# Two-layer hybrid trunk on one core: dense moving operands at the bottom of SBUF, weights at its top

## The chip, the cores and the metric

One core of a Trainium2 chip runs the whole program in one launch. The metric is the device time of one execution in microseconds (us). A measurement of the kernel before is the median of 3 runs; a profiled execution is one run more, with a time of its own.

TensorE multiplies a stationary operand (at most 128x128, loaded by LDWEIGHTS) with a moving operand (128 partitions by 512 columns here) into an accumulator in PSUM. VectorE (DVE), ScalarE (ACT) and GpSimd (POOL) do the elementwise work; SyncE (SP) issues the transfers from HBM. SBUF is the working memory of 128 partitions. In this text a place in SBUF is a distance from the bottom of a partition, in KB of 1024 bytes.

## What is computed

T = 512 tokens, width 1024, two layers. Each adds a mixer's output to the residual and then a gated feed-forward block of inner width 2816:

```python
def swiglu(xn, w_gu, w_down):
    gate, up = jnp.split(xn @ w_gu, 2, axis=-1)
    return (jax.nn.silu(gate) * up) @ w_down
...
for layer in range(DEPTH):
    xn = rms_norm(x, norm_mix[layer])
    h = even_mixer(xn, ...) if layer % 2 == 0 else odd_mixer(xn, ...)
    x = x + h
    x = x + swiglu(rms_norm(x, norm_ffn[layer]), ffn_w_gu[layer], ffn_w_down[layer])
```

The even mixer (layer 0) is a short convolution and a chunked gated delta rule; the odd one (layer 1) is a recurrence with 8 heads and an attention part with low-rank queries and values. All is in 32-bit floats.

## The kernel before

**Dense products.** Everything is kept transposed: features on the partitions, tokens on the columns. A weight block of up to 8 x 128 rows by 128 columns is fetched into `wraw` by `Core.weight`, and split into a high part `whi` (rounded to fp32r) and a low part `wlo` (the rest), 512 columns at a time, four buffers of each. An activation is split in the same way into hi and lo. `Core.mm` makes each 128-deep step of a product of three fp32r matmuls: hi by `whi`, lo by `whi`, hi by `wlo`. The weight is the stationary operand and the activation the moving one, with one exception: in the value product of the attention part the weight block moves, and a 128x128 slice of the activation (`f`) is stationary.

**Activations.** `Core.big` hands out tiles of [128, 8, 512] words (16 KB a partition), four in all; a normalized activation takes a pair of them, hi and lo (`norm_begin`), and the mixers use them for other things too. In a feed-forward block one pair holds the block's input and the other is idle until the last down product.

**Feed-forward block (`Core.ffn`).** The 22 inner units of 128 rows go in two halves of 11. For each unit: gate and up, 8 steps of 3 matmuls each; VectorE and ScalarE make silu(gate) x up, and split it into `hi` and `lo`, each a ring of 13 tiles of [128, 512] in the block's own pool. Then the down product of this half: for each of 8 output blocks, 11 steps of 3 matmuls, added to the residual `xres`. Gate and up are thus 1056 matmuls a layer and down is 528. `mixer_out` ahead of it makes the mixer's output projection and `xres`.

**Order.** `Plan` predicts when each operand is ready and which engine is free, and the recorded operations are issued in that order (line 242, `emit`, which is why most operations of VectorE and ScalarE stand at L242 in the profile; matmuls stand at L363, transposes at L367, transfers at L315). It knows sizes and engines, and no addresses.

**Places.** Pools are stacked from the bottom of SBUF in the order in which they are opened: constants (`con`), weights (`wp`), activations (`act`), and on top of these one pool for each phase (`gdn`, `ffn0`, `odd`, `ffn1`), which is freed at the phase's end. In the built program that gives, in KB, with the places after the change beside them:

| tiles | before | after |
|---|---|---|
| `whi`, `wlo` (stationary) | 30 to 46 | 179 to 195 |
| the four `big` tiles (moving) | 46 to 94 and 114 to 130 | 16 to 80 |
| `x2k` (working tiles of DVE and ACT) | 94 to 112 | 195 to 213 |
| phase pools, from | 133 | 80 |
| `hi` and `lo` of the inner units (moving) | 153 to 205 | the idle `big` pair, and 80 to 100 |
| `xres` | 133 to 149 | 100 to 116 |
| `f` of the attention part | 166 to 224 | 112 to 170 |
| `bones` (a constant matrix, stationary) | 138 | 84 |
| `wraw` | 22 to 30 | 171 to 179 |

The input pair of the feed-forward block lies before at 62 to 78 KB (hi) and 114 to 130 KB (lo) in layer 0, and at 46 to 62 KB (hi) and 78 to 94 KB (lo) in layer 1.

Of the kernel before, what the change touches and what calls it, by code (L numbers as in the profile page):

```python
# [8 lines left out]
F32 = mybir.dt.float32  # L9
F32R = mybir.dt.float32r  # L10
I32 = mybir.dt.int32
AF = mybir.ActivationFunctionType
OP = mybir.AluOpType
# [3 lines left out]
T = 512  # L17
D = 1024
KD = D // 128
D_FF = 2816  # L20
KF = D_FF // 128
# [4 lines left out]
class Plan:  # L26
# [6 lines left out]
    def __init__(self, known):  # L33
        self.now = self.started = 0.0
        self.cols = set(range(4))
        self.busy = {e: ([], []) for e in ("V", "A", "G", "D")}
        self.uses, self.last, self.base, self.slots = {}, {}, {}, {}
        self.known = known
        self.keys, self.seen = {}, {}
        self.dense = []  # L40
        self.place = {}
        self.floor = {}
        self.writes, self.reads = {}, {}
# [209 lines left out]
class Core:  # L253
# [4 lines left out]
    def __init__(self, ctx, tc, I, O, first):  # L258

        self.ctx, self.tc, self.nc, self.I, self.O, self.first = ctx, tc, tc.nc, I, O, first  # L260
        self.pools, self.lined, self.odd_row = {}, [], None
        self.plan = Plan(first.plan.seen if first else None)
        self.con = self.pool(ctx, "con")
        self.wp = self.pool(ctx, "wp")
        self.act = self.pool(ctx, "act")
        self.dr = self.pool(ctx, "dr", space=bass.MemoryType.DRAM)
        self.ps = self.pool(ctx, "ps", space=PSUM)
        self.pp, self.banks = None, {}
        self.V, self.A, self.G = (Engine(self, e, n) for e, n in ((self.nc.vector, "V"), (self.nc.scalar, "A"), (self.nc.gpsimd, "G")))
        self.E = Engine(self, None, "E")  # L270
        self.held, self.flying, self.live, self.ops = {}, 0, [], []
        self.cur, self.steps = Stream(None, None, ()), {}
        self.n = 0
        self.fed = KF

    def pool(self, ctx, name, **kw):
        p = ctx.enter_context(self.tc.tile_pool(name=name, bufs=1, **kw))
        self.pools[id(p)] = name
        if not kw and name not in ("gdn", "odd"):
            self.lined.append(p)  # L280
        self.plan.floor[name] = self.plan.end()
        return p
# [5 lines left out]
    def tile(self, pool, shape, dt, tag, bufs=1, name=None, typed=False):  # L288

        cur = self.cur  # L290
        cur.tiles += 1
        slot = (self.pools[id(pool)], tag)
        n = int(np.prod(shape[1:]))
        full = [shape[0], -(-n // self.ROW) * self.ROW] if pool in self.lined and tag not in ("x2k", "half") and n % self.ROW else shape

        def make(i):

            t = pool.tile(full, dt, name=name or self.nm(tag), **({"tag": f"{tag}{i}", "bufs": 1} if typed else {"tag": tag, "bufs": bufs}))[:]
            if full is not shape:
                t = t[:, :n]  # L300
                if len(shape) == 3:
                    t = t.rearrange("p (a b) -> p a b", b=shape[2])
                elif len(shape) == 4:
                    t = t.rearrange("p (a b c) -> p a b c", b=shape[2], c=shape[3])
            return t

        t = self.plan.alloc(slot, bufs, (cur.key, cur.tiles), make, lambda old: self.live and (not typed or old.dtype == dt))
        if self.live and not self.first:
            need = self.steps.setdefault((cur.key, cur.step), {})
            need[slot] = (min(need.get(slot, (0, 0))[0] + 1, bufs), bufs)  # L310
        return t if t.dtype == dt else t.bitcast(dt)
# [11 lines left out]
        else:  # L323
            instr()

    def line(self, pool):

        return self.tile(pool, [128, 8], F32, "half")

    def const(self, name):  # L330
        return self.tile(self.con, list(self.I[name].shape), F32, "c_" + name)

    def big(self, dt=F32):
        return self.tile(self.act, [128, KD, T], dt, "big", 4, typed=True)

    def x2k(self, dt=F32, full=False):
        t = self.tile(self.act, [128, T + 4], dt, "x2k", self.NX)
        if not self.odd_row:
            self.odd_row = self.line(self.act)
        return t if full else t[:, :T]  # L340


# [260 lines left out]
        return rs, self.col  # L603


    def ffn(self, fp, l, xs, xres, done):
        I, V, A = self.I, self.V, self.A
        half = KF // 2
        for f0 in (0, half):
            hs = []  # L610
            for f in range(f0, f0 + half):
                pg = self.do(self.project(I["w_gu"][l, 2 * f], xs, tag="mf"))
                pu = self.do(self.project(I["w_gu"][l, 2 * f + 1], xs, tag="mf"))
                if f == 0:
                    rs, _ = self.do(self.norm_end("mm"))
                g, u, h = self.x2k(), self.x2k(), self.x2k()
                V.tensor_tensor(g, pg, rs[:], op=OP.mult)
                A.activation(g, g, AF.Silu)
                V.tensor_tensor(u, pu, rs[:], op=OP.mult)
                V.tensor_tensor(h, g, u, op=OP.mult)  # L620
                hi = self.tile(fp, [128, T], F32R, "hi", 13)
                lo = self.tile(fp, [128, T], F32R, "lo", 13)
                A.activation(hi[:], h, AF.Copy)
                V.tensor_tensor(lo[:], h, hi[:], op=OP.subtract)
                hs.append((hi[:], lo[:]))
            for c in range(KD):
                ps = self.bank("mf")
                for a, b in ((0, 8), (8, half)):
                    w = self.weight(I["w_down"][l, c][:, (f0 + a) * 128:(f0 + b) * 128], b - a, 128)
                    self.do(self.mm(ps, w, hs[a:b], first=a == 0, last=b == half))  # L630
                V.tensor_tensor(xres[:, c], ps, xres[:, c], op=OP.add)
                if f0:
                    done(c, xres[:, c])
# [1229 lines left out]
def build(tc, I, O):  # L1863
    program(tc, I, O, program(tc, I, O, None))


def program(tc, I, O, first):
    with ExitStack() as ctx:
        c = Core(ctx, tc, I, O, first)
        resid, part = (c.dr.tile([KD, 128, T], F32, name=n) for n in ("resid", "part"))  # L1870

        def mixer_out(fp, l, w, ys, old):

            xres = c.tile(fp, [128, KD, T], F32, "xres")
            xs = c.norm_begin(gf[:, KD * l:KD * l + KD])
            for k in range(KD):
                ps = c.do(c.project(w[k], ys, kt=len(ys), tag="mf", late=k < 2))
                x = c.tile(fp, [128, T], F32, "xold", 2)
                c.dma(x, old[k])
                c.V.tensor_tensor(xres[:, k], ps, x, op=OP.add)  # L1880
                c.norm_add(k, xres[:, k])
            return xres, xs

        gm, c.ident, c.ones, c.mhalf, c.stack, gf = (c.const(n) for n in ("norm_mix", "ident", "ones", "mhalf", "stack", "norm_ffn"))
        c.dma(gm, I["norm_mix"])
        c.G.memset(c.ones, 1.0)
        c.A.activation(c.mhalf, c.ones[:, 0:1], AF.Copy, scale=-0.5)
        ys = c.even(gm[:, 0:KD], {"ident": c.ident, "stack": c.stack, "norm_ffn": gf})
        with ExitStack() as fx:
            fp = c.pool(fx, "ffn0")  # L1890
            c.phase(fx, "ffn0", mf=6)
            xres, xs = mixer_out(fp, 0, I["w_eo"], ys, I["xT"])
            c.rope_tables()
            nxt = []

            def done(k, x):
                if k == 0:
                    nxt.append(c.norm_begin(gm[:, KD:2 * KD]))
                c.norm_add(k, x)
                c.dma(resid[k], x)  # L1900

            c.ffn(fp, 0, xs, xres, done)
        xs = nxt[0]
        ys = c.odd(xs, resid, part)
        with ExitStack() as fx:
            fp = c.pool(fx, "ffn1")
            c.phase(fx, "ffn1", mf=6)
            xres, xs = mixer_out(fp, 1, [I["w_oo"][k][:, 0:512] for k in range(KD)], ys, part)
            c.ffn(fp, 1, xs, xres, lambda k, x: c.dma(O["outT"][k], x))
    return c  # L1910


# [12 lines left out]
```

## Time and profile before

| | us |
|---|---|
| median of 3 runs | 1413.68 |
| lowest and highest | 1409.71, 1416.58 |
| the profiled execution, its own time | 1414.12 |
| its span, from the first to the last instruction | 1412.3 |

How to read it: TensorE is busy for 1351.1 us of the span (96%), VectorE for 869.2, ScalarE for 539.4, GpSimd for 248.3. A matmul's recorded duration overlaps the next one's, and its end is modelled; the interval from one start to the next is read from the timeline. In the names of matmuls, `mfps<-big,whi` is: accumulator, moving operand, stationary operand. `mfps` are the accumulators of the feed-forward phases, `mmps` and `mxps` those of the mixers.

### The profile page before, as it was taken

Reading aid. Unit: us, or ns where it says so; the run is one execution under the profiler, and the core shown is the slowest. Engines: PE = TensorE matmul, PEld = TensorE weight load, DVE = VectorE, ACT = ScalarE, POOL = GpSimd, SP = SyncE. Lnnn points to the kernel's source line nnn. Section 1 sums busy time; section 2 is a strip of 40 time slices with the busy share of each in tenths; the row PEclk is TensorE's granted clock in tenths of the full one; section 3 lists DMA queues with packets and bytes.
Section 4 is the critical chain, followed back from the end, with each engine's and each line's share of the span. In section 5 each row is a group of like instructions: output and inputs, shape, how many; then the busy total and the mean of one; then the engine's idle time right before and its main releaser. Section 6 shows DMA issues by size and latency. Waiting matters only on the chain.

```text
span 1412.3 us, 19643 instructions
## 1 busy us (share of the span) xinstructions
PE 1351.1 (96%) x7526; PEld 1076.5 (76%) x7526; DVE 869.2 (62%) x1653; ACT 539.4 (38%) x1003; POOL 248.3 (18%) x221
## 2 busy tenths in 40 slices
PE   8987899999999999999988979998999999999998
PEld 5766788788888888888756757775688888888887
DVE  6999887656444344444699986786755443344432
ACT  5332454243333233334334244635654332233321
POOL 2456132120000000001234541441020000000000
PEclk9999999999999999999989999999999999999999
DMA  5122011242332332324411220155242232322232
GB/s 162 53 68 75 31 61 57 93 156 90 93 102 82 98 104 90 104 86 133 131 46 60 86 69 24 55 169 166 97 165 90 90 96 87 105 100 94 91 119 84
DMA packets 52799, 132.91 MB, mean 94 GB/s; under 512 B 7520, under 2 KB 15712, under 8 KB 52704
## 3 DMA queue, kind: packets, MB, share of 16 engines
q1 hardware_dynamic: 52704, 131.65, 29.1%
q8 instruction: 59, 0.97, 0.3%
q14 instruction: 36, 0.29, 0.1%
HBM read 121.14 MB, written 10.49 MB: 93 GB/s over the span
## 4 chain that ended last, share of the span: by engine, by line
PE 76%; DVE 16%; ACT 3%; issue 2%; POOL 1%; DMA 1%; SPq 0%; POOLq 0%; DVEq 0%; ACTq 0%
PE mfps L363 56%; PE mmps L363 12%; PE mxps L363 7%; DVE x2k L242 6%; DVE big L242 3%; DVE mem L242 2%; PE mxps L367 2%; ACT x2k L242 1%; DVE ar L242 1%; DVE bk L242 1%; DVE wlo L242 1%; DVE f L242 1%; POOL mem L242 1%; ACT mem L242 1%; DMA big<-in_xT 0%
## 5 line engine op out<-in xcount | busy, mean ns | idle before, releaser
L363 PE MATMUL mfps<-big,whi 128*128 128x512 f32 x1600 | 495.0, 390 | 0.6 <-DVE big L242 0.6
L242 ACT ACTIVATE whi<-wraw 128x512 fp32r<-128x512 f32 (+1 forms) x384 | 238.5, 622 | 517.7 <-PE mfps L363 416.3
L242 DVE TENSOR_TENSOR wlo<-wraw,whi 128x512 fp32r<-128x512 f32 (+1 forms) x344 | 234.1, 681 | 214.4 <-ACT whi L242 212.3
L363 PEld LDWEIGHTS mfps<-big,whi 128*128 128x128 f32 x1600 | 300.3, 188 | 64.9 <-DVE big L242 0.9
L363 PE MATMUL mfps<-big,wlo 128*128 128x512 f32 x800 | 311.4, 390 | 1.5 <-DVE wlo L242 1.5
L363 PE MATMUL mmps<-big,whi 128*128 128x512 f32 x768 | 256.3, 415 | 4.6 <-DVE x2k L242 4.6
L363 PEld LDWEIGHTS mfps<-big,wlo 128*128 128x128 f32 x800 | 150.2, 188 | 34.1 <-DVE wlo L242 1.9
L363 PEld LDWEIGHTS mmps<-big,whi 128*128 128x128 f32 x768 | 139.3, 194 | 38.4 <-issue 9.9
L363 PE MATMUL mmps<-big,wlo 128*128 128x512 f32 x384 | 152.9, 398 | 0.0
L363 PE MATMUL mfps<-lo,whi 128*128 128x512 f32 x352 | 139.0, 395 | 0.0
L363 PE MATMUL mfps<-hi,wlo 128*128 128x512 f32 x352 | 139.0, 395 | 0.0
L363 PE MATMUL mfps<-hi,whi 128*128 128x512 f32 x352 | 138.9, 395 | 0.0
L242 DVE TENSOR_TENSOR x2k<-mfps,rs 128x512 f32<-128x512 f32 x88 | 60.6, 691 | 126.6 <-PE mfps L363 124.2
L242 POOL TENSOR_TENSOR wlo<-wraw,whi 128x512 fp32r<-128x512 f32 x70 | 94.3, 1353 | 129.6 <-ACT whi L242 83.4
L242 POOL TENSOR_TENSOR sqacc<-x2k,sqacc 128x512 f32<-128x512 f32 x21 | 27.6, 1316 | 430.1 <-issue 308.8
L363 PEld LDWEIGHTS mmps<-big,wlo 128*128 128x128 f32 x384 | 73.9, 192 | 17.0
L363 PEld LDWEIGHTS mfps<-lo,whi 128*128 128x128 f32 x352 | 66.0, 187 | 16.1
L363 PEld LDWEIGHTS mfps<-hi,whi 128*128 128x128 f32 x352 | 66.0, 188 | 16.1
L363 PEld LDWEIGHTS mfps<-hi,wlo 128*128 128x128 f32 x352 | 66.0, 188 | 16.1
L242 ACT ACTIVATE x2k<-x2k 128x512 f32<-128x512 f32 x79 | 49.9, 631 | 66.5 <-DVE x2k L242 57.3
L367 PE MATMUL mxps<-c_ident,x2k 128*128 128x128 f32 (+1 forms) x196 | 34.6, 288 | 19.5 <-DVE x2k L242 17.7
L242 DVE TENSOR_TENSOR xres<-mfps,xres 128x512 f32<-128x512 f32 x32 | 22.1, 690 | 47.4 <-PE mfps L363 47.4
(311 smaller groups left out, 1555.7 us busy)
## 6 DMA issues: line engine op xcount, KB each, us to landing
wraw<-in_w_gu SPq DMA_DIRECT2D x88, 512.0 KB, 3.5
wraw<-in_w_down SPq DMA_DIRECT2D x32, 512.0 KB, 3.4
wraw<-in_w_ev SPq DMA_DIRECT2D x30, 512.0 KB, 3.5
wraw<-in_w_od SPq DMA_DIRECT2D x20, 512.0 KB, 3.5
wraw<-in_w_down SPq DMA_DIRECT2D x32, 192.0 KB, 2.3
wraw<-in_w_eo SPq DMA_DIRECT2D x8, 512.0 KB, 3.6
wraw<-in_w_oo SPq DMA_DIRECT2D x16, 256.0 KB, 3.0
big<-in_xT SPq DMA_DIRECT2D x8, 256.0 KB, 6.1
```

The lines of the kernel that those rows point to most:

```text
L242: c.emit(t, lambda: getattr(eng, op)(*a, **kw))
L363: self.emit(t, lambda: self.nc.tensor.matmul(out, lhsT, rhs, **kw))
L367: self.emit(t, lambda: self.nc.tensor.transpose(out, x, ident))
```

## The change

Four edits, all of which move tiles:

1. A pool `mov` is opened first, at the bottom of SBUF, and holds the four `big` tiles. Constants, activations and weights go to the other end (`side="right"`), the weights lowest there.
2. The inner units' rings `hi` and `lo` are no tiles of their own any more. Of their 13 places, the first 8 are the slices of the idle `big` pair and 5 are slices of a new tile `hid` in the block's pool, one for hi and one for lo.
3. `hid` is made in `mixer_out`, before `xres`, so that it lies at the bottom of the block's pool.
4. A filler row next to the `x2k` tiles goes away.

```diff
-        self.con = self.pool(ctx, "con")
-        self.wp = self.pool(ctx, "wp")
-        self.act = self.pool(ctx, "act")
+        self.mov = self.pool(ctx, "mov")
+        self.con = self.pool(ctx, "con", side="right")
+        self.act = self.pool(ctx, "act", side="right")
+        self.wp = self.pool(ctx, "wp", side="right")
...
     def big(self, dt=F32):
-        return self.tile(self.act, [128, KD, T], dt, "big", 4, typed=True)
+        return self.tile(self.mov, [128, KD, T], dt, "big", 4, typed=True)
...
-    def ffn(self, fp, l, xs, xres, done):
+    def ffn(self, fp, l, xs, xres, more, done):
         I, V, A = self.I, self.V, self.A
-        half = KF // 2
+        half, ring = KF // 2, KD + 5
+        hid = [[t[:, k] for k in range(KD)] for t in (self.big(F32R), self.big(F32R))]
+        for part, t in zip(hid, more):
+            part += [t[:, k] for k in range(ring - KD)]
...
-                hi = self.tile(fp, [128, T], F32R, "hi", 13)
-                lo = self.tile(fp, [128, T], F32R, "lo", 13)
-                A.activation(hi[:], h, AF.Copy)
-                V.tensor_tensor(lo[:], h, hi[:], op=OP.subtract)
-                hs.append((hi[:], lo[:]))
+                hi, lo = (part[f % ring] for part in hid)
+                A.activation(hi, h, AF.Copy)
+                V.tensor_tensor(lo, h, hi, op=OP.subtract)
+                hs.append((hi, lo))
...
         def mixer_out(fp, l, w, ys, old):
 
+            more = [c.tile(fp, [128, 5, T], F32R, "hid", 2) for _ in range(2)]
             xres = c.tile(fp, [128, KD, T], F32, "xres")
```

The order of the instructions stays. On TensorE, at the first down product of layer 0, from the last matmul of the last up product on, there stood before (numbers tell buffers apart):

```order
L363 MATMUL mfps_5955<-big_4722,wlo_5964 128x512
L363 MATMUL mfps_6001<-hi_5187,whi_6004 128x512
L363 MATMUL mfps_6001<-lo_5188,whi_6004 128x512
L363 MATMUL mfps_6001<-hi_5187,wlo_6006 128x512
L363 MATMUL mfps_6001<-hi_5268,whi_6004 128x512
```

and there stands now:

```order
L358 MATMUL mfps_5864<-big_4649,wlo_5873 128x512
L358 MATMUL mfps_5908<-big_5023,whi_5911 128x512
L358 MATMUL mfps_5908<-big_5024,whi_5911 128x512
L358 MATMUL mfps_5908<-big_5023,wlo_5913 128x512
L358 MATMUL mfps_5908<-big_5023,whi_5911 128x512
```

Each inner unit is read at the same turn; only the tile that holds it has another name, here one `big` tile for all the hi parts and one for the lo parts. (The lines are shifted by 5, since lines went away above.)

## Rows read from the trace of the kernel before

**Rows 1.** The page's first lines, and its part 4.

```profile
span 1412.3 us, 19643 instructions
PE 1351.1 (96%) x7526; PEld 1076.5 (76%) x7526; DVE 869.2 (62%) x1653; ACT 539.4 (38%) x1003; POOL 248.3 (18%) x221
...
PE 76%; DVE 16%; ACT 3%; issue 2%; POOL 1%; DMA 1%; SPq 0%; POOLq 0%; DVEq 0%; ACTq 0%
PE mfps L363 56%; PE mmps L363 12%; PE mxps L363 7%; DVE x2k L242 6%; DVE big L242 3%; DVE mem L242 2%; PE mxps L367 2%; ACT x2k L242 1%; DVE ar L242 1%; DVE bk L242 1%; DVE wlo L242 1%; DVE f L242 1%; POOL mem L242 1%; ACT mem L242 1%; DMA
```

**Rows 2.** Chain of waits in order of time: start us, us, what, matmuls.

```profile
278.55 50.33 PE mfps L363 x220
337.35 347.31 PE mfps L363 x1507
1021.80 33.34 PE mfps L363 x144
1062.82 345.86 PE mfps L363 x1510
```

**Rows 3.** The page's part 5: groups by line and shape.

```profile
L363 PE MATMUL mfps<-big,whi 128*128 128x512 f32 x1600 | 495.0, 390 | 0.6 <-DVE big L242 0.6
...
L363 PEld LDWEIGHTS mfps<-big,whi 128*128 128x128 f32 x1600 | 300.3, 188 | 64.9 <-DVE big L242 0.9
...
L363 PE MATMUL mfps<-lo,whi 128*128 128x512 f32 x352 | 139.0, 395 | 0.0
```

**Rows 4.** Timeline of TensorE, gate and up, layer 1: start us, us, what, count.

```profile
1099.64 0.61 PE L363 MATMUL mfps<-big,whi 128*128 128x512 f32 x2
...
1139.77 0.61 PE L363 MATMUL mfps<-big,whi 128*128 128x512 f32 x2
```

**Rows 5.** The same view, gate and up, layer 0.

```profile
379.78 0.39 PE L363 MATMUL mfps<-big,wlo 128*128 128x512 f32 x1
...
419.83 0.39 PE L363 MATMUL mfps<-big,whi 128*128 128x512 f32 x1
```

**Rows 6.** The same view, a down product, layer 0.

```profile
449.76 0.39 PE L363 MATMUL mfps<-lo,whi 128*128 128x512 f32 x1
...
489.89 0.39 PE L363 MATMUL mfps<-hi,wlo 128*128 128x512 f32 x1
```

**Rows 7.** The same view, the value product of the attention part.

```profile
944.48 0.39 PE L363 MATMUL mmps<-wlo,f 128*128 128x512 f32 x1
944.72 0.63 PE L363 MATMUL mmps<-whi,f 128*128 128x512 f32 x2
...
947.98 0.39 PE L363 MATMUL mmps<-wlo,f 128*128 128x512 f32 x1
```

**Rows 8.** The same view, two pairs of both far.

```profile
792.74 0.64 PE L363 MATMUL mxps<-f,bones 128*128 128x512 f32 x2
793.23 0.63 PE L363 MATMUL mxps<-big,whi 128*128 128x512 f32 x2
...
800.68 0.63 PE L363 MATMUL mxps<-f,bones 128*128 128x512 f32 x2
801.15 0.63 PE L363 MATMUL mxps<-big,whi 128*128 128x512 f32 x2
```

**Rows 9.** The tile hi: what ACT and DVE do, min/median/max ns.

```profile
L242 ACT ACTIVATE hi<-x2k x44: 616/632/635, 340.8 to 1349.0; 128x512 fp32r<-128x512 f32 x44
L242 DVE TENSOR_TENSOR lo<-x2k,hi x44: 684/692/693, 341.5 to 1349.7; 128x512 fp32r<-128x512 f32 x44
```

**Rows 10.** Timeline of TensorE, short runs in the two mixers.

```profile
178.74 0.62 PE L363 MATMUL mmps<-big,whi 128*128 128x512 f32 x2
...
180.58 0.39 PE L363 MATMUL mmps<-big,wlo 128*128 128x512 f32 x1
...
938.05 0.39 PE L363 MATMUL mmps<-f,wlo 128*128 128x512 f32 x1
...
940.13 0.40 PE L363 MATMUL mmps<-f,wlo 128*128 128x512 f32 x1
```

More of the change, by code (lines that the diff above doesn't have):

```diff
@@ L260, in __init__ @@
         self.ctx, self.tc, self.nc, self.I, self.O, self.first = ctx, tc, tc.nc, I, O, first
-        self.pools, self.lined, self.odd_row = {}, [], None
+        self.pools, self.lined = {}, []
         self.plan = Plan(first.plan.seen if first else None)
-        self.con = self.pool(ctx, "con")
-        self.wp = self.pool(ctx, "wp")
-        self.act = self.pool(ctx, "act")
+        self.mov = self.pool(ctx, "mov")
+        self.con = self.pool(ctx, "con", side="right")
+        self.act = self.pool(ctx, "act", side="right")
+        self.wp = self.pool(ctx, "wp", side="right")
         self.dr = self.pool(ctx, "dr", space=bass.MemoryType.DRAM)
@@ L278, in pool @@
         self.pools[id(p)] = name
-        if not kw and name not in ("gdn", "odd"):
+        if "space" not in kw and name not in ("gdn", "odd"):
             self.lined.append(p)
@@ L293, in tile @@
         n = int(np.prod(shape[1:]))
-        full = [shape[0], -(-n // self.ROW) * self.ROW] if pool in self.lined and tag not in ("x2k", "half") and n % self.ROW else shape
+        full = [shape[0], -(-n // self.ROW) * self.ROW] if pool in self.lined and tag not in ("x2k",) and n % self.ROW else shape
         def make(i):
@@ L324, in emit @@
             instr()
-    def line(self, pool):
-        return self.tile(pool, [128, 8], F32, "half")
     def const(self, name):
@@ L333, in big @@
     def big(self, dt=F32):
-        return self.tile(self.act, [128, KD, T], dt, "big", 4, typed=True)
+        return self.tile(self.mov, [128, KD, T], dt, "big", 4, typed=True)
     def x2k(self, dt=F32, full=False):
         t = self.tile(self.act, [128, T + 4], dt, "x2k", self.NX)
-        if not self.odd_row:
-            self.odd_row = self.line(self.act)
         return t if full else t[:, :T]
@@ L1881, in mixer_out @@
                 c.norm_add(k, xres[:, k])
-            return xres, xs
+            return xres, xs, more
         gm, c.ident, c.ones, c.mhalf, c.stack, gf = (c.const(n) for n in ("norm_mix", "ident", "ones", "mhalf", "stack", "norm_ffn"))
@@ L1891, in program @@
             c.phase(fx, "ffn0", mf=6)
-            xres, xs = mixer_out(fp, 0, I["w_eo"], ys, I["xT"])
+            xres, xs, more = mixer_out(fp, 0, I["w_eo"], ys, I["xT"])
             c.rope_tables()
@@ L1900, in done @@
                 c.dma(resid[k], x)
-            c.ffn(fp, 0, xs, xres, done)
+            c.ffn(fp, 0, xs, xres, more, done)
         xs = nxt[0]
@@ L1907, in program @@
             c.phase(fx, "ffn1", mf=6)
-            xres, xs = mixer_out(fp, 1, [I["w_oo"][k][:, 0:512] for k in range(KD)], ys, part)
-            c.ffn(fp, 1, xs, xres, lambda k, x: c.dma(O["outT"][k], x))
+            xres, xs, more = mixer_out(fp, 1, [I["w_oo"][k][:, 0:512] for k in range(KD)], ys, part)
+            c.ffn(fp, 1, xs, xres, more, lambda k, x: c.dma(O["outT"][k], x))
     return c
```

## The prediction

> **What bounds the kernel now.** Read the page's first and fourth parts first [rows 1]. TensorE is busy for 96% of a span of 1412.3 us, and 76% of the chain of work that ended last is TensorE's. Of that chain, 56% is `mfps`, the accumulators of the two feed-forward blocks and of the two output projections, and 12% is `mmps`, the dense products of the two mixers. Next read the chain in order of time [rows 2]. Two pieces of it are nothing but matmuls: 1507 of them in 347.31 us (layer 0) and 1510 in 345.86 us (layer 1). No other engine and no transfer ends a wait inside either, so in half of the span the time is the number of matmuls times the interval from the start of one to the start of the next. The change keeps the number. Only the interval can move, and that is the quantity to read.
>
> The groups by line give a mean duration of 390 ns to a product with `big` moving and of 395 ns to one with `lo` moving [rows 3]. These durations overlap and their ends are modelled, so they are a hint, not the interval. The timeline of TensorE gives it: take the start of a first and a last row of an unbroken stretch and divide by the matmuls between. Four stretches, all 128x128 by 128x512 in fp32r:
>
> - gate and up of layer 1, moving operands at 46 to 62 KB (hi) and 78 to 94 KB (lo), stationary at 30 to 46 KB: 177 matmuls from 1099.64 to 1139.77, **226.7 ns** each [rows 4].
> - gate and up of layer 0, moving at 62 to 78 KB (hi) and 114 to 130 KB (lo), stationary the same: 175 from 379.78 to 419.83, **228.9 ns** [rows 5].
> - the down product, moving at 153 to 205 KB, stationary the same: 172 from 449.76 to 489.89, **233.3 ns** [rows 6].
> - the value product of the attention part, where the roles are turned round: weights of 30 to 46 KB move, and a slice of `f` at 210 to 220 KB is stationary: 15 from 944.48 to 947.98, **233.3 ns** [rows 7].
>
> I read these so. A dense product whose two operands both lie low takes 226.7 ns; one far operand, of whichever kind, adds 6.6 ns; 228.9 is what comes out when one matmul in three (the lo part) has a far operand, 226.7 + 6.6/3 = 228.9. The border for the moving operand lies between 94 KB, the top of the highest tile that is cheap, and 114 KB. The fourth stretch decides the forecast, because it is the only place where a far stationary operand meets a low moving one for long, and it costs as much as the far moving operand of the third. There is one weaker sign that the two add: the pairs `f,bones` have both operands far (165 KB and more, 138 KB), and two of them take 0.47 and 0.49 us, 235 and 245 ns each [rows 8].
>
> **The change part by part.** The program's instructions are the same, in the same order on every engine; the inner units' tiles have other names, and three instructions of TensorE that only wait, ahead of the first down product, are gone. The down product stands between matmuls without idle time [rows 2], so I cost these at nothing. So the change is a change of places, and there are three kinds.
>
> *The moving operands go down.* `big` lies at 16 to 80 KB, the inner units at 16 to 100 KB (eight of 13 in the idle `big` pair, five in the new tile). All but the last 6 KB are below the 94 KB that are known to be cheap, and those hold the lo parts of three of the 22 inner units, which move in one down matmul of three: 1056/3 x 3/22, 48 matmuls, 0.3 us at most.
>
> *The weights go up.* `whi` and `wlo` move from 30 to 46 KB to 179 to 195 KB. Every dense product loads one of them, so by the fourth stretch each of them pays 6.6 ns. The two moves meet in the down product: the moving operand's 6.6 ns is given back and the stationary one's is taken, 233.3 before and after, gain nothing. In gate and up there is little or nothing to give back, and 6.6 ns to pay.
>
> *The rest.* `x2k` goes up by 101 KB, the phase pools down by 53 KB, for VectorE and ScalarE. Such an operation takes 684 to 693 ns for `lo` and 616 to 635 for `hi` [rows 9]; these spreads of 9 and 19 ns are the room that I give to a place. In the two long pieces such work is hidden behind the matmuls [rows 2], and in the mixers, where the two moves have opposite signs, I take 0, with 1 us either way.
>
> The sum, with 233.3 ns as the interval of each dense product afterwards and 0.39 us for the last matmul of a piece:
>
> - layer 0's long piece: 1506 x 233.3 ns + 0.39 = 351.7 us against 347.31, **+4.4**.
> - layer 1's: 1509 x 233.3 + 0.39 = 352.4 against 345.86, **+6.6**.
> - the output projections' pieces [rows 2]: 219 x 233.3 + 0.39 = 51.5 against 50.33, **+1.2**; 143 x 233.3 + 0.39 = 33.8 against 33.34, **+0.4** (here lo and hi already lie far in part).
> - the mixers: 12% of the chain, 169 us, is `mmps`, at 0.23 us each some 740 matmuls. They stand in short runs after a wait, and there the interval has not settled: with both operands low, 8 matmuls from 178.74 to 180.58 take 230.0 ns each; with a far moving operand, 9 from 938.05 to 940.13 take 231.1 [rows 10]. So the price is between 1.1 ns (0.8 us) and the settled 6.6 ns (4.9 us). The rows nearest to such runs give the lower end, and longer ones come nearer to the upper, so I stay below the middle: **+2.0**.
>
> Together +14.6 us. The profiled execution took 1414.12 us, the median of the runs is 1413.68; on the median that gives **1428.3 us**, 1.0% slower. Three bounds go into the range: the mixers, 0.8 to 4.9 us; the interval after the change, read over 3.50 us with starts to 0.01 us, good to 0.7 ns, which is 2 us over 3015 matmuls; and the products of the attention part with `f`, in which both operands are then far, 120 matmuls, 0.8 us. With the 1 us of the other engines the forecast's own range is 1424 to 1434.
>
> [...]
>
> **The rivals.** [...]
>
> *The place counts for nothing*, and the intervals come from something that the change leaves alone: which accumulator is written, which tile is filled meanwhile, or the order of the three products. Then the time stays at **1413.7 us**. [...] Against it: rows 4 and 5 are the same code on the same shapes with the same engines at work, and differ in the place of the two moving tiles alone.
>
> That the tiles don't go where the change says is excluded by the built program's addresses; that the inner units make a new wait is excluded by its order, since their 13 places are reused in the same turn as before.
>
> **How the numbers follow.** I give the forecast 0.78, the first rival 0.14, the second 0.08. What a measurement of this kernel can tell from no change is about 0.5%, 7 us: the forecast's whole own range (10 us and more above) counts as slower, the first rival (9.7 below) as faster, the second as the same. The range reaches from the forecast down over the second rival to 1412 and up to 1434; it leaves out the first rival and some of the tails, about 0.18.
>
> **What would show it.** Right: the two long pieces of the chain measure some 351.7 and 352.4 us; the mean of `mfps<-big,whi` rises from 390 to about 395 ns while products of the inner units stay at 394 to 396; the timeline of layer 1's gate and up gives 233.3. Wrong: gate and up at 226.7 or less and inner units at 389 or 390 mean that only moving operands count; layer 0 at 228.9 still, with the down product at 233.3, means that places don't count. A new wait in either long piece would mean that the turn of the inner tiles does bind. If gate and up settle between 227 and 233, the price of a far stationary operand was mis-sized.

## The result, and the profile after

The changed kernel takes 1427.87 us (median of 6 runs, 1427.57 to 1429.68), the kernel before 1415.32 us (6 runs, 1409.71 to 1416.74): ratio 1.0096, 95% interval 1.0078 to 1.0114, so 1.0% slower. The forecast was 1428.3 us. The number came out, and so did most terms of its sum. The reason given for it did not: in the experiments below it is not the place of an operand that costs (with the weights as far away, but 64 B lower, the kernel takes 1406.16 us).

The page of the kernel after, its first lines and part 4, against [rows 1]:

```profile
span 1425.8 us, 19643 instructions
PE 1368.5 (96%) x7526; PEld 1078.1 (76%) x7526; DVE 871.8 (61%) x1653; ACT 539.9 (38%) x1003; POOL 249.4 (17%) x221
...
PE 78%; DVE 15%; ACT 3%; issue 2%; DMA 1%; POOL 1%; SPq 0%; POOLq 0%; DVEq 0%; ACTq 0%
```

As many instructions, 13.5 us more span, 17.4 us more recorded busy time on TensorE, the other engines within 3 us of where they were. The granted clock is 0.985 in this execution and 0.986 in that of the kernel before, so the clock is not what changed. The chain of waits of the kernel after, the pieces that answer to [rows 2] (start us, us, what, matmuls):

```profile
279.10 51.60 PE mfps L358 x220
...
339.25 351.63 PE mfps L358 x1507
...
1028.35 33.60 PE mfps L358 x144
...
1069.80 352.34 PE mfps L358 x1510
```

The pieces hold the same numbers of matmuls, so no new wait cuts them. They grew by 1.27, 4.32, 0.26 and 6.48 us, together 12.3 of the 13.5 us. The groups by line and shape, against [rows 3]:

```profile
L358 PE MATMUL mfps<-big,whi 128*128 128x512 f32 x2112 | 664.3, 396 | 0.6 <-DVE big L242 0.6
L358 PEld LDWEIGHTS mfps<-big,whi 128*128 128x128 f32 x2112 | 396.9, 188 | 96.3 <-DVE big L242 0.9
...
L358 PE MATMUL mfps<-hid,whi 128*128 128x512 f32 x192 | 60.7, 396 | 0.0
```

The mean of the products with `big` moving rose from 390 to 396 ns, the load's stayed at 188. The timeline of TensorE after the change (start us, us, what, count) gives the interval: gate and up of layer 1, then of layer 0, then down, then the value product, against [rows 4 to 7]:

```profile
1099.73 0.39 PE L358 MATMUL mfps<-big,wlo 128*128 128x512 f32 x1
...
1139.63 0.40 PE L358 MATMUL mfps<-big,wlo 128*128 128x512 f32 x1
```

```profile
379.68 0.40 PE L358 MATMUL mfps<-big,wlo 128*128 128x512 f32 x1
...
419.58 0.39 PE L358 MATMUL mfps<-big,wlo 128*128 128x512 f32 x1
```

```profile
449.91 0.63 PE L358 MATMUL mfps<-hid,whi 128*128 128x512 f32 x2
...
489.81 0.63 PE L358 MATMUL mfps<-hid,whi 128*128 128x512 f32 x2
```

```profile
950.90 0.39 PE L358 MATMUL mmps<-wlo,f 128*128 128x512 f32 x1
...
954.40 0.39 PE L358 MATMUL mmps<-wlo,f 128*128 128x512 f32 x1
```

171 products in the first three pairs (39.90 us each) and 15 in the last (3.50): 233.3 ns everywhere. The last was the first thing that did not fit. Both its operands now lie far (179 KB and more, and above 112 KB), one more than before, and it still takes 233.3 ns.

Intervals given below are worked out in this way, as the mean over settled triples of the trace; a triple is the three products of one step, hi by `whi`, lo by `whi`, hi by `wlo`.

### The profile page after: what moved, and what is told of

Its sections match the earlier page's. It is cut to its first block, busy times and chain, and to the rows that moved or that the text cites. A ratio compares the mean times of both kernels' runs of the same rounds, so it can differ in the third digit from the quotient of the medians.

```text
span 1425.8 us, 19643 instructions
## 1 busy us (share of the span) xinstructions
PE 1368.5 (96%) x7526; PEld 1078.1 (76%) x7526; DVE 871.8 (61%) x1653; ACT 539.9 (38%) x1003; POOL 249.4 (17%) x221
## 4 chain that ended last, share of the span: by engine, by line
PE 78%; DVE 15%; ACT 3%; issue 2%; DMA 1%; POOL 1%; SPq 0%; POOLq 0%; DVEq 0%; ACTq 0%
PE mfps L358 56%; PE mmps L358 14%; PE mxps L358 7%; DVE x2k L242 6%; DVE big L242 3%; DVE mem L242 2%; PE mxps L362 2%; ACT x2k L242 1%; DVE ar L242 1%; DVE f L242 1%; DVE bk L242 1%; ACT mem L242 1%; DMA qd<-x2k 0%; DMA big<-in_xT 0%; DVE wlo L242 0%
## 5 line engine op out<-in xcount | busy, mean ns | idle before, releaser
L358 PE MATMUL mfps<-big,whi 128*128 128x512 f32 x2112 | 664.3, 396 | 0.6 <-DVE big L242 0.6
L358 PEld LDWEIGHTS mfps<-big,whi 128*128 128x128 f32 x2112 | 396.9, 188 | 96.3 <-DVE big L242 0.9
L358 PE MATMUL mfps<-big,wlo 128*128 128x512 f32 x1056 | 417.5, 396 | 1.4 <-DVE wlo L242 1.4
L358 PEld LDWEIGHTS mfps<-big,wlo 128*128 128x128 f32 x1056 | 198.5, 188 | 49.5 <-DVE wlo L242 1.8
L242 ACT ACTIVATE x2k<-x2k 128x512 f32<-128x512 f32 x79 | 49.9, 632 | 64.8 <-DVE x2k L242 55.5
L358 PE MATMUL mfps<-hid,whi 128*128 128x512 f32 x192 | 60.7, 396 | 0.0
L242 DVE SCALAR_TENSOR_TENSOR x2k<-x2k,conv_qkv,x2k 128x512 f32<-128x512 f32 x54 | 49.9, 924 | 1.6
L362 PEld LDWEIGHTS mxps<-c_ident,x2k 128*128 128x128 f32 (+1 forms) x196 | 23.1, 142 | 33.5 <-DVE x2k L242 23.0
L358 PEld LDWEIGHTS mfps<-hid,whi 128*128 128x128 f32 x192 | 36.1, 188 | 8.7
L242 DVE TENSOR_TENSOR big<-x2k,big 128x512 fp32r<-128x512 f32 x36 | 26.9, 746 | 20.5 <-ACT big L242 20.3
L242 DVE TENSOR_TENSOR x2k<-x2k,x2k 128x512 f32<-128x512 f32 x52 | 37.7, 726 | 1.2 <-ACT x2k L242 1.1
```

Source lines behind the costliest of these rows:

```text
L242: c.emit(t, lambda: getattr(eng, op)(*a, **kw))
L358: self.emit(t, lambda: self.nc.tensor.matmul(out, lhsT, rhs, **kw))
L362: self.emit(t, lambda: self.nc.tensor.transpose(out, x, ident))
```

## The experiments

**Are both operands low enough?** The changed kernel with the weights in a pool of their own at 80 to 96 KB, and `hid` behind it at 96 to 116 KB.

```diff
         self.mov = self.pool(ctx, "mov")
+        self.wst = self.pool(ctx, "wst")
-            hi = self.tile(self.wp, [128, 512], F32R, "whi", 4)
+            hi = self.tile(self.wst, [128, 512], F32R, "whi", 4)
-            lo = self.tile(self.wp, [128, 512], F32R, "wlo", 4)
+            lo = self.tile(self.wst, [128, 512], F32R, "wlo", 4)
```

> The changed kernel with one edit: whi and wlo come from a pool of their own at 80 to 96 KB, just above the big tiles; wraw stays high. Theory (a far operand, the stationary one as well, costs 6.6 ns): gate and up settle at 226.7 ns in both layers, the two long pieces of the chain fall to 341.8 and 342.5 us, and the time is about 1404 us, 24 below the changed kernel and 10 below the kernel before. The down product settles between 226.7 and 233.3: hid now lies at 96 to 116 KB, and its five units of thirteen tell on which side of that the border lies. Rival (weights' place does not count, the 233.3 of the changed kernel comes from the moving operands' new place at the bottom): gate and up stay at 233.3 and the time at 1428 us.

Measured: 1405.49 us (6 runs), ratio to before 0.9932, interval 0.9914 to 0.9950: faster than either kernel. The chain of waits of this kernel, its two long pieces:

```profile
338.62 341.62 PE mfps L359 x1507
...
1057.09 342.32 PE mfps L359 x1510
```

(341.62 - 0.39) / 1506 is 226.6 ns: gate, up and down all run at the short interval, the slices of `hid` at 114 to 116 KB too. This looked like proof of the place. It is also what two other things give, as it turned out.

**Do the weights' places alone make the loss?** The kernel before with its weights' pool on the right, at 208 KB and up; the moving tiles slide down by 24 KB.

```diff
-        self.wp = self.pool(ctx, "wp")
+        self.wp = self.pool(ctx, "wp", side="right")
-        if not kw and name not in ("gdn", "odd"):
+        if "space" not in kw and name not in ("gdn", "odd"):
```

> The kernel before with one edit: the weights' pool alone goes to the top (whi and wlo at 208 to 224 KB); everything else moves down by 24 KB, hi and lo of the inner units lie at 129 to 181 KB. Theory with prices that add: gate and up 233.3 ns, down product 240.0 (both operands far), 1435 us. Theory with one price for a product, whichever of its operands is far: gate and up 233.3, down 233.3, about 1428 us. Rival (the distance between the two operands counts, not the place): gate and up 233.3, but the down product, whose operands are now 27 to 95 KB apart, 227 to 229, about 1420 us.

Measured: 1427.85 us (4 runs), ratio 1.0087, interval 1.0070 to 1.0104: the whole loss. Its two long pieces:

```profile
339.02 351.63 PE mfps L363 x1507
...
1069.10 352.35 PE mfps L363 x1510
```

These are the changed kernel's to 0.01 us, though here the down product has both operands far and there only one. So, in terms of places, a second far operand costs nothing: the prices do not add.

**One weight half low, the other high.** Two runs from the changed kernel, the pool `wst` of the first experiment for `whi` alone, or for `wlo` alone.

```diff
-            hi = self.tile(self.wp, [128, 512], F32R, "whi", 4)
+            hi = self.tile(self.wst, [128, 512], F32R, "whi", 4)
```

> The changed kernel with whi at 80 to 88 KB and wlo left high: one matmul in three has a far stationary operand. If each matmul pays for its own far operand: 226.7 + 6.6/3 = 228.9 ns in gate and up, time about 1413 us. If one far operand in a stretch holds up all three: 233.3 and 1428 us.

> The changed kernel with wlo at 80 to 88 KB and whi left high: two matmuls in three have a far stationary operand. If each matmul pays for its own: 226.7 + 2 x 6.6/3 = 231.1 ns in gate and up, time about 1421 us. If one far operand in a stretch holds up all three: 233.3 and 1428 us.

Measured: 1418.99 us with `whi` low and 1423.18 with `wlo` low (one run each; before's median in the same session 1415.31). The piece of layer 0 in the first, and in the second:

```profile
339.81 348.31 PE mfps L359 x1507
```

```profile
339.00 348.31 PE mfps L359 x1507
```

Both settle at 231.1 ns, whether one load in three is far or two (the 4.2 us between the two runs lie outside the long pieces). A price per far product gives that for two of three, not for one. In these two runs a triple has an interval of its own, which is not the mean of its three products.

**Where is the border?** Two runs. In one the weights lie across the 116 KB that the runs so far suggested, behind the activation tiles, with `whi` from 106016 B and `wlo` from 114208 B. In the other only `hid` is shifted, by 10 KB against the kernel with all low, its low parts to 118912 B and up.

```diff
-        self.act = self.pool(ctx, "act", side="right")
+        self.act = self.pool(ctx, "act")
+        self.wst = self.pool(ctx, "wst")
```

(and `whi` and `wlo` in it, as above)

> The changed kernel, but the weight tiles whi and wlo lie in a pool of their own right after the activation tiles, so that the four whi tiles begin at 106016, 108064, 110112 and 112160 B and the four wlo tiles at 114208, 116256, 118304 and 120352 B; hid comes behind them and lies far, and big and its inner units low as in the changed kernel. Theory (the weight load has the same border as the moving operand, about 116 KB): matmuls whose loaded tile begins at 116256 B or more have a far load, so triples of three of every four steps that share a wlo tile slot, have one far load of three; gate and up come out between the 226.7 ns of all near and the 231.1 ns of one far load in three, about 229 to 230 ns averaged, and the run near 1412 to 1417 us. Rival (the load's border lies elsewhere): below 106 KB, everything 233.3 ns and about 1427 us; between 106 and 114 KB, between 231.1 and 233.3 ns; above 122 KB, gate and up 226.7 ns and about 1406 to 1408 us, since only the down products of hid stay slower.

```diff
+            c.tile(fp, [128, 5, T], F32, "pad")
             more = [c.tile(fp, [128, 5, T], F32R, "hid", 2) for _ in range(2)]
```

> The kernel with all operands low, but with 10 KB unused ahead of hid, whose high parts then lie at 106.1 to 116.1 KB and its low parts from 118912 B up, beyond the border read from the runs so far; the weights stay low. Theory (a moving operand beyond about 116 KB is far): the down triples of the 5 hid units of 22, with one far moving operand of three, go from 226.7 to about 228.9 ns, all else stays at 226.7; that is 192 x 5 / 22 or some 60 triples of 2.2 ns x 3 each a layer, under 1 us in all, so 1405 to 1407 us, and the cadence tells, not the time. Rival (the border lies beyond 126 KB or counts by something else than the address): hid stays at 226.7 ns.

Measured: 1426.03 us and 1405.86 us (one run each, before 1416.45). The first has gate and up at 233.3 ns throughout; the second has `hid` at 226.7 ns up to 126 KB. The groups of the products with `hid` moving, of the first and of the second:

```profile
L359 PE MATMUL mfps<-hid,whi 128*128 128x512 f32 x192 | 60.5, 395 | 0.0
```

```profile
L359 PE MATMUL mfps<-hid,whi 128*128 128x512 f32 x192 | 59.4, 389 | 0.0
```

Both answers went against the theory. Weights from 104 KB up are slow (233.3 ns), moving tiles at 116 to 126 KB are fast (226.7), while in the kernel before moving tiles at 114 KB were slow (228.9) [rows 5]. No border at an address gives that, and the theory of the place was given up. What is left of an address when the place is taken away is its low bits. All fast tiles in all kernels started at a multiple of 128 B (`big` 16512 or 47104 B, weights 82048 or 30720 B), every slow combination had one that did not (117184, 182976, 106016 B).

**Does a start off a multiple of 128 B cost?** Three runs. The column rows `rscol` keep their 32 B, by which, in the kernel before, everything behind them comes 64 B lower and, in the changed one, the weights 64 B higher; in both all tiles then start at multiples of 128 B. The third is the kernel with all low, with the weights (and `hid`) pushed 64 B off, and `rscol` as in the other two.

```diff
-        full = [shape[0], -(-n // self.ROW) * self.ROW] if pool in self.lined and tag not in ("x2k", "half") and n % self.ROW else shape
+        full = [shape[0], -(-n // self.ROW) * self.ROW] if pool in self.lined and tag not in ("x2k", "half", "rscol") and n % self.ROW else shape
```

> The kernel before, but the column rows rscol keep their 32 B each instead of 64 B, so that everything behind them lies 64 B lower: the fourth big tile begins at 117120 B instead of 117184, the inner units from 157056 B on instead of 157120, and all of them now begin at multiples of 128 B, as the near ones always did. Nothing else moves. Theory of the start address (an fp32r operand that begins off a multiple of 128 B costs 6.7 ns a product, wherever it lies): every settled stretch at 226.7 ns, the layer 1 feed-forward piece of the chain 345.9 - 960 x 3 x (228.9 - 226.7) ns = about 341 us with what the down products give back, and 1402 to 1407 us in all. Theory of the place (beyond about 116 KB costs): 64 B change nothing, gate and up 226.7 and 228.9 ns, down 233.3 ns, 1412 to 1417 us.

> The changed kernel with the same edit: rscol lies at the far end of SBUF among the activation rows, and the weights' pool below it rises by 64 B, whi to 183040 B and wlo to 191232 B, both multiples of 128 B, as far away as in the changed kernel. Theory of the start address: 226.7 ns in every settled stretch, layer 0 and layer 1 pieces near 340 us as with all operands low, 1403 to 1408 us. Theory of the place: 233.3 ns throughout and 1426 to 1430 us.

```diff
+        self.gap = self.pool(ctx, "gap")
         self.wst = self.pool(ctx, "wst")
...
+        c.tile(c.gap, [128, 16], F32, "gap")
```

> The kernel with all operands low, but with 64 B unused between the big tiles and the weights, so that whi and wlo begin at 82112 B and 90304 B, 64 B past multiples of 128, as low as before; hid is moved by 64 B with them. Theory of the start address: 233.3 ns in gate and up and in the output projections, 233.3 ns or less in down, 1424 to 1430 us. Theory of the place: 226.7 ns and 1403 to 1409 us.

Measured: 1419.19 us (10 runs, ratio 1.0025, interval 1.0016 to 1.0035), 1427.65 us (5 runs, 1.0080, 1.0055 to 1.0105) and 1426.62 us (one run). The third came out as the start address would have it: 64 B turn a fast kernel, all low, 1405.49 us, into a slow one. The first two did not. With the weights far and at a multiple of 128 B the interval is 232.4 ns, not 226.7 and no longer 233.3; in the kernel before, layer 0's gate and up, at 228.9 ns, went to 231.1 in the first half and to 233.3 in the second. The piece of layer 0 in the first, where it was 347.31 us [rows 2], and in the second:

```profile
339.76 350.10 PE mfps L363 x1507
```

```profile
339.47 350.20 PE mfps L358 x1507
```

The timeline of the first, in the two halves of layer 0's gate and up:

```profile
379.81 0.39 PE L363 MATMUL mfps<-big,wlo 128*128 128x512 f32 x1
...
419.33 0.40 PE L363 MATMUL mfps<-big,wlo 128*128 128x512 f32 x1
...
559.53 0.39 PE L363 MATMUL mfps<-big,wlo 128*128 128x512 f32 x1
...
599.43 0.39 PE L363 MATMUL mfps<-big,wlo 128*128 128x512 f32 x1
```

171 products lie between the rows of each pair: 39.52 us, 231.1 ns each, and 39.90 us, 233.3 ns each. The tiles, their places and the order of the products are the same in both halves, so one set of addresses has two settled intervals here.

So low bits do count, but neither start by itself. What the numbers have in common is the **distance** from the start of the loaded tile to the start of the moving tile: in each kernel that is fast (226.7 ns) it is a multiple of 512 B (16512 and 82048 B are both 128 past one), which is called in step from here on; in the kernel before and after, the products at 228.9 or 233.3 ns have one at 448 past, in these two, those at 231.1 to 233.3 ns have one at 384.

**Offsets by themselves.** A program of nothing but products, with both starts varied at four pairs of places.

```python
for u in (0, 120 * KB):                 # loaded tiles
    for v in (32 * KB, 152 * KB):       # moving tiles
        for s in OFF:
            for m in OFF:
                chain(n % 8, [(u + s + 512 * (i % 8), v + m + 2 * KB * (i % 8)) for i in range(REP)])
```

> A program that leaves out the whole computation and only times products: chains of 14 fp32r products of 512 columns, each with its own 128 x 128 weight load, with the loaded tiles at 16 KB or 136 KB and the moving tiles at 48 KB or 168 KB, and each of the two 0, 4, 16, 32, 48, 64, 96 or 112 B past a multiple of 128 B; then triples in the kernel's pattern with each of its four tiles at 0 or at 32 or 64 B past it. Theory of the start address: offset 0 on both sides 226.7 ns in all four places, any 64 B offset on either side 233.3 ns, on both sides still 233.3 ns; triples with the low weight alone off 231.1 ns and with the high weight alone off 231.1 ns, with the low moving tile alone off 228.9 ns. Theory of the place: 226.7 ns with both low, 233.3 ns where either lies at 136 KB or 168 KB, whatever the offset.

Measured: chains of 14 are short (runs of 8 and 9 products stood at 230.0 and 231.1 ns in the kernel before [rows 10]), so their values are compared with each other alone. Two readings stand. The last three of the four pairs of places give the same 64 values to 0.2 ns, low or high: the place has no part in these. (The first pair differs in its first 19 chains alone; the next experiment tells why.) And of the triples, over their last 18 products, those with all four tiles in step, unshifted or all shifted, by 32 or by 64 B, take 226.7 to 228.1 ns, all others 228.9 to 234.4.

**The changed kernel, its weights as far away but in step.** One pair of 32 B rows goes from the attention part's pool to the activation pool; the weights come 64 B lower, to 182912 and 191104 B.

```diff
-                    rk = tl([8], "rkc", bufs=2)
+                    rk = self.tile(self.act, [128, 8], F32, "rkc", 2)
```

(and `rkc` is left unrounded, as `x2k` is).

> The changed kernel with one 64 B pair of small rows (rkc) moved from the attention part's pool to the activation pool, by which the weights' pool lies 64 B lower: whi from 182912 B, wlo from 191104 B, 66 KB and more above every moving tile as in the changed kernel, but now a whole number of 512 B from the big and hid tiles (16512 B and 82048 B on; all are 128 B past a multiple of 512). Theory of the step (what counts is the distance between the start of the loaded tile and of the moving tile, modulo 512 B or a smaller power of two above 128 B: a multiple is 226.7 ns, anything else locks into 232 to 233.3 ns): 226.7 ns in every settled stretch of gate, up and down, layer 1 piece of the chain near 340 us, 1403 to 1408 us in all. Theory of the place: 233.3 ns and 1426 to 1430 us. Theory that nothing but a start at a multiple of 128 B or less counts: fallen already with the 232.4 ns of the weights at 183040 B; it would give 232 to 233 ns and 1425 to 1429 us here too.

Measured: 1406.16 us (10 runs, 1403.73 to 1412.57), ratio to before 0.9944, interval 0.9924 to 0.9964. The chain of waits of this kernel, the four pieces, and a group:

```profile
277.93 50.17 PE mfps L358 x220
...
336.50 341.62 PE mfps L358 x1507
...
1016.98 32.65 PE mfps L358 x144
...
1057.35 342.32 PE mfps L358 x1510
```

```profile
L358 PE MATMUL mfps<-big,whi 128*128 128x512 f32 x2112 | 650.5, 389 | 0.6 <-DVE big L242 0.6
L358 PEld LDWEIGHTS mfps<-big,whi 128*128 128x128 f32 x2112 | 396.3, 188 | 83.1 <-DVE big L242 0.9
```

The weights lie more than 78 KB above every moving tile of the feed-forward blocks (102528 B is the top of `hid`), and the four pieces are those of the kernel with all low, to 0.01 us. 64 B take the two long pieces from 351.63 to 341.62 and from 352.34 to 342.32 us.

**The distance by itself.** The program of products with chains of 48, at three pairs of places, from two starts.

```python
for u, v in PLACES:      # (low, low), (low, high), (high, low)
    for s in (0, 64):
        for d in APART:
            chain(n % 8, [(u + s + 512 * (i % 8), v + s + d + 2 * KB * (i % 8)) for i in range(REP)])
```

> A program that leaves out the whole computation and only times products: chains of 48 fp32r products of 512 columns with a 128 x 128 load each, at three pairs of places (loaded tiles at 16 KB with moving tiles at 48 KB or at 168 KB, loaded tiles at 136 KB with moving tiles at 48 KB), the loaded tiles 0 or 64 B past a multiple of 128 B, and the moving tiles' start modulo 512 B further by 0, 16, 32, 64, 96, 128, 192, 256, 320, 384, 448, 480, 512, 576, 768 or 1024 B. Theory of the step: over the last 24 products of a chain 226.7 ns at 0, 512 and 1024 B in all three pairs of places and both starts, 232 to 233.3 ns at 64, 96, 384, 448 and 480 B, the distances of the real kernels; 576 B as 64 B, and 256 and 768 B alike, whichever it is (226.7 ns if the modulus is 256 B). Theory of the place: the row of the first pair 226.7 ns throughout, the others 233.3 ns throughout.

Measured: the timeline of TensorE in it, one row for the products of a chain that fall into one window (start us, us to the end of the last, what, count). Loaded tiles low, moving tiles high, start 64 B; the distances are 0, 64, 128, 192, 256, 384, 448 and 1024 B:

```profile
562.04 5.60 PE L118 MATMUL acc<-place 128*128 128x512 f32 x24
...
595.51 5.43 PE L118 MATMUL acc<-place 128*128 128x512 f32 x23
...
617.58 5.76 PE L118 MATMUL acc<-place 128*128 128x512 f32 x24
...
628.78 5.76 PE L118 MATMUL acc<-place 128*128 128x512 f32 x24
...
639.85 5.60 PE L118 MATMUL acc<-place 128*128 128x512 f32 x24
...
661.86 5.75 PE L118 MATMUL acc<-place 128*128 128x512 f32 x24
...
673.04 5.76 PE L118 MATMUL acc<-place 128*128 128x512 f32 x24
...
728.12 5.60 PE L118 MATMUL acc<-place 128*128 128x512 f32 x24
```

Take 0.39 us for the last product and divide by one less: 226.5, 229.1, 233.5, 233.5, 226.5, 233.0, 233.5 and 226.5 ns. From starts over the last 24 products of each chain, in ns:

```
distance B       0    16    32    64    96   128   192   256
all six      226.7 231.7 233.3 228.9 233.3 233.3 233.3 226.7

distance B     320   384   448   480   512   576   768  1024
all six      228.9 232.3 233.3 233.3 226.7 228.9 226.7 226.7
```

All six series agree to 0.1 ns, whatever the places and the start. The multiples of 256 B tried (0, 256, 512, 768 and 1024) take 226.7 ns. 384 B gives 232.3 and 128 B 233.3, so the values as a whole do not repeat after 256 B; after 512 B those tried do (512 and 1024 B as 0, 576 as 64, 768 as 256).

The first series has to be counted off with care. In the order of the source it seems to have 233.3 ns at 0 B, 228.9 at 16 and 226.7 at 64 and 96. The built program issues its first 387 products in another order. TensorE starts while ScalarE still fills `place`, from the bottom up:

```profile
12.88 1.65 PE L118 MATMUL acc<-place 128*128 128x512 f32 x3 [12.88 <-ACT place L113]
```

```profile
54.38 1.14 ACT L113 ACTIVATE place<-raw 128x512 fp32r<-128x512 f32 x2
```

The chain that the source has first, 48 products ahead of those shown, reads the top of `place`, so it can't be the one that starts at 12.88 us. By the order of the built program the first chains are interleaved, and the unbroken runs of one distance in them, of 41 products or more each, end on the table's values too.

Stretches of real kernels in which the three products of a step have the same distance, beside this table (distance modulo 512 B, worked out from the tiles' starts; interval measured in the kernel):

| kernel, products | distance | table | kernel |
|---|---|---|---|
| before, gate and up of layer 1 | 0 | 226.7 | 226.7 |
| before, down; value product | 448 | 233.3 | 233.3 |
| after, all feed-forward | 448 | 233.3 | 233.3 |
| all low; far but in step | 0 | 226.7 | 226.7 |
| before with weights high | 32, 480 | 233.3 | 233.3 |
| weights from 104 KB, gate and up | 96 | 233.3 | 233.3 |
| before 64 B lower, down | 384 | 232.3 | 232.8 |
| after, weights 64 B higher | 384 | 232.3 | 232.4 |
| all low, weights 64 B off, gate and up | 448 | 233.3 | 233.3 |

Where `hid` is in step but stands among `big` out of step, nine products in a row, it takes between the two: 230.0 to 231.5 ns, by step, with the weights from 104 KB. So nine products were not enough to settle there, which may be why short runs stood between as well, 8 products at 230.0 and 9 at 231.1 ns [rows 10].

## Why the prediction was right, and where its reason was wrong

- *The interval is the quantity, and 233.3 ns what it becomes.* Held. Forecast for the long pieces were 351.7 and 352.4 us, measured 351.63 and 352.34; for the projections 51.5 and 33.8, measured 51.60 and 33.60.
- *The mixers, +2.0 us.* Mis-sized: 13.5 - 12.3 leaves 1.2 us for all the rest, near the lower end given, 0.8. The base was off the other way: with the 1415.32 us of 6 runs in place of the 1413.68 of 3, the same sum would have given 1429.9. The two nearly cancel, so that 1428.3 met 1427.87 this closely is in part luck.
- *"One far operand, of whichever kind, adds 6.6 ns."* This is the step that failed. The four stretches on which it rested [rows 4 to 7] differ in place and in distance modulo 512 B at once: 0 in the first, 448 for the lo part of the second, 448 in the third and 448 in the fourth. The change happens to put all feed-forward products at 448 as well (16512 and 82048 against 182976 B), so what was measured in the fourth stretch came back. That is luck. Had the pools ended 64 B lower, the same change by the same words would have made 1406.16 us, and the forecast would have been 22 us off.
- *"One weaker sign that the two add."* Fell: both far is 233.3 ns in the value product after, and in the down product with the weights high. The 0.8 us for the attention part were not paid. The pairs `f,bones` at 235 and 245 ns [rows 8] are two products each, between others; nothing here shows that they had settled.
- *The first rival, that only the moving operand's place counts.* Fell as a mechanism: between the changed kernel and the one in step no moving tile of the feed-forward blocks changes its place, and 64 B of the weights' start make 22 us (1427.87 against 1406.16). At 226.7 ns throughout it would have given 341.8 and 342.5 us for the long pieces; those are the figures of the kernels in step, 341.62 and 342.32, since 226.7 ns is the interval there too.
- *The place counts for nothing.* True as far as the runs go, as the kernel far but in step shows (1406.16 us, with all low 1405.49), and yet the time did not stay: the change leaves places and low bits joined. The argument against it, that rows 4 and 5 differ "in the place of the two moving tiles alone", overlooked the low bits of the same addresses.
- *The load.* The recorded load of the feed-forward products stays at 187 to 188 ns, in the kernel before [rows 3], in the one after and in the one in step, shorter than any interval. Still, the interval moves between 226.7 and 233.3 ns with nothing but the distance between the starts of the loaded and the moving tile.
- *Other engines.* The program of products has no other engine at work in its chains from 55.5 to 1010.9 us and shows the same intervals, 226.7 to 233.3 ns, so no other engine is needed for it.

What the chip does inside is not settled: no run shows why the values repeat after 512 B, nor whether the distance that counts is that to a product's own loaded tile or to the next one's, since neighbours have the same distance modulo 512 B in all these stretches. Nor is the mixed triple settled: one third or two thirds of the loads at 448 B both gave 231.1 ns, one third of the moving tiles 228.9; with one third of the moving tiles at 384 B, as in the kernel before 64 B lower, it was 231.1 in one half of layer 0 and 233.3 in the other. What went before may count there too; how is open.

## What to carry to other kernels

Where the settled interval of back-to-back fp32r products differs between stretches of the same shape, read the tiles' start addresses down to the byte: loaded and moving tiles a multiple of 256 B apart ran at 226.7 ns for 512 columns here, the other distances tried at 228.9 to 233.3. One 64 B row, a rounding of small tiles, decided it here for the whole program (1427.87 against 1406.16 us), so pad pools in front of such tiles, and look at the distances again after every edit of a pool. A price read from a few stretches is a price of everything in which they differ; before a cause is written down, list what else is different, and move the suspected thing by an amount that changes nothing else. And before a row of a trace is given to a line of the source, make sure in which order the built program issues it.

## What was not expected of the hardware

- The place of an operand in SBUF, 16 to 184 KB, did not change the interval by 0.2 ns in the program of products; 64 B of distance did by 6.6 ns (226.7 at 256 B, 233.3 at 192 B).
- Starts that were both shifted by the same 64 B kept their interval to 0.1 ns; only their distance changed it, and the interval never settled above 233.3 ns at the distances tried in chains of 48.
- An interval took products to settle: nine in a row at distance 0, among others at 96 B, came to 230.0 ns and more, not to 226.7, with the weights from 104 KB. And with one third of the moving tiles at 384 B the same addresses settled on two values, 231.1 and 233.3 ns.
